# A top-16 search of score columns moved into the query stage of a routed expert layer, and where its row dot products are written

## The chip, the cores and the metric

One core of a Trainium2 chip runs the kernel alone. The metric is the device time of one execution in microseconds, as the median of several runs.

## What is computed

Two transformer-like blocks run over 512 tokens of width 1024. The change lies in the feed-forward part of the first: 8 heads, each with two sets of 128 sub-keys, choose 16 of 16384 one-neuron experts per token.

```python
s1 = einsum('chd,hkd->chk', q[..., :128], keys1)   # scores on 128 keys
s2 = einsum('chd,hkd->chk', q[..., 128:], keys2)
v1, i1 = top_k(s1, 16)
v2, i2 = top_k(s2, 16)
cand = (v1[..., :, None] + v2[..., None, :]).reshape(..., 256)
sc, ci = top_k(cand, 16)
idx = i1[ci // 16] * 128 + i2[ci % 16]
g = softmax(sc)
act = gelu(einsum('chkd,cd->chk', peer_u[idx], h)) * g
out = einsum('chk,chkd->cd', act, peer_v[idx])
```

Everything is float32. A product is formed as three matmuls of operands split into a high and a low part.

## The kernel before

**Tiles and paths.** The tokens form four tiles of 128, t = 0 to 3. Tile 0 takes a sparse path: for each of its 128 (head, choice) pairs an indirect DMA issued by POOL (L1118) gathers one row of `peer_u` per token into a ring of six row tiles, DVE forms the dot product with the token's activations (L1127, a row product and a read of the accumulator), and after a gelu the same is done with rows of `peer_v`, which DVE adds up into `sacc` (L1138). Tiles 1 to 3 (384 tokens) take a dense path through all 16384 experts.

**Stage one, blocks u0 to u127** (`experts_in`). Each block takes 128 experts. SP loads a weight tile `wraw` (512 KB, L225, three buffers), ACT rounds it to `whi` (L268), DVE subtracts to get `wlo` (L269; called the split below), PE does 24 matmuls of 384 columns (L274 to L276), ACT applies the gelu into a tile `A` (L1171), and every second block ACT issues the store of the pair to `adram` (L1173). `A` has three buffers and holds two blocks; eight columns behind them (`hold`) carry the row indices that POOL reads for its gathers.

**Query stage, ahead of u0** (`query`). Sixteen chunks c0 to c15, one per head and half: PE makes a chunk of the queries and then multiplies it with the keys for the four token tiles; ACT copies the scores into `sall` (L1155).

**Routing** (`route(t)`). For each tile: the top 16 of each of 16 score columns, five DVE operations each (L1187 to L1191, called a search below, 64 in all); sums of candidates and their own top 16; softmax; decoding of the indices. For t = 0 the result is `sidx`, the list of rows to gather. For t = 1 to 3 follow 32 items per tile, 96 in all, that make the gate matrix: DVE compares (`O`, L1292) and multiplies twice (L1297), ACT copies, PE does eight matmuls into `pG` (L1301), ACT copies the result into `G` (L1303). After every eighth item ACT stores 2 MB of `G` to `gdram` (L1305).

**Stage two, blocks v0 to v127** (`phase_p2`). `fetch_ag(g)` has SP load 8 blocks of `A` and of `G` (1.5 MB each; `G` shares two buffers with the tiles of the routing). DVE multiplies them (L1341, 128 instructions), ACT and DVE split the product (`ahl`), and PE accumulates it with the rows of `peer_v` in 18 matmuls of 512 columns per block.

**What sets the order.** Every engine works through one static list. A scheduler makes the lists from the order in which the program emits its work, and `phase_p1` sets that by a budget: each u-block adds 4.6 to `have`; the searches and the rest of tile 0's routing take first; once they are done, each block calls `some(1.24)`, which advances the sparse path by 1.24 rows, and then steps of the routing of tiles 1 to 3 until the budget is spent.

```python
have += 4.6
while have > 0 and (d := next(first, None)) is not None:
    have -= d
if have > 0:
    self.some(1.24)
    have -= 1.45
    while have > 0 and left:
        d = next(rest, None)
```

Of the kernel before, what the change touches and what calls it, by code (L numbers as in the profile page):

```python
# [12 lines left out]
F32 = mybir.dt.float32  # L13
# [3 lines left out]
U32 = mybir.dt.uint32  # L17
AF = mybir.ActivationFunctionType
OP = mybir.AluOpType
# [8 lines left out]
TT = S // 128  # L28
SD = S - 128
# [175 lines left out]
class Stream:  # L205
# [38 lines left out]
    def next(self, held=0):  # L244

        n = self.n_used
        self._split(n + 1 + self.ahead - held)
        self.n_used += 1
        return self.got.pop(n)


class Kernel:
# [806 lines left out]
    def phase_p1(self):  # L1059
        nc, pp = self.nc, self.pp  # L1060

        ring = self.p0.tile([128, 4, D], F32, name="ring", tag="xres")
        more = pp.tile([128, 2, D], F32, name="ring2")
        self.ring = [ring[:, j] for j in range(4)] + [more[:, j] for j in range(2)]
        self.hs = pp.tile([128, D], F32, name="hs")
        nc.gpsimd.dma_start(out=self.hs, in_=self.hdram)

        self.iota2 = pp.tile([128, 128, 2], F16, name="iota2")
        nc.vector.tensor_copy(self.iota2, self.iota[:, :, None].to_broadcast([128, 128, 2]))
        self.iota16 = pp.tile([128, 16, 16], BF16, name="iota16")  # L1070
        nc.vector.tensor_copy(self.iota16, self.iota[:, :16, None].to_broadcast([128, 16, 16]))
        self.query()
        self.AG = {}
        first, rest, dense = self.route(0), chain(*(self.route(t) for t in range(1, TT))), self.experts_in()
        self.sparse = self.sparse_experts()

        have = 0.0
        left = True
        for n, _ in enumerate(dense):
            have += 4.6  # L1080
            while have > 0 and (d := next(first, None)) is not None:
                have -= d
            if have > 0:
                self.some(1.24)
                have -= 1.45
                while have > 0 and left:
                    d = next(rest, None)
                    left = d is not None
                    have -= d or 0.0
                have = min(have, 0.0)  # L1090
            if n >= 120 and not left and not self.AG:
                self.fetch_ag(0)
        for _ in chain(first, rest):
            pass
# [8 lines left out]
    def sparse_experts(self):  # L1103

        nc, pp = self.nc, self.pp
        v = nc.vector
        dots = pp.tile([128, 128], F32, name="dots")
        src = [self.a["peer_r"], self.a["peer_v"].rearrange("a b d -> (a b) d")]
        R = len(self.ring)

        def fetch(n):

            if n < 256:
                ix = self.sidx[:, n % 128:n % 128 + 1]
                if n >= R - 1:
                    v.tensor_copy(self.hold[0], ix)  # L1116
                    ix = self.hold.pop(0)
                nc.gpsimd.indirect_dma_start(  # L1118
                    out=self.ring[n % R], out_offset=None, in_=src[n // 128],
                    in_offset=bass.IndirectOffsetOnAxis(ap=ix, axis=0))  # L1120

        for n in range(R - 1):
            fetch(n)
        for n in range(128):
            fetch(n + R - 1)
            r = self.ring[n % R]
            v.tensor_tensor_reduce(r, r, self.hs, 1.0, 0.0, op0=OP.mult, op1=OP.add, accum_out=dots[:, n:n + 1])  # L1127
            yield
        nc.scalar.activation(dots, dots, AF.Gelu)
        v.tensor_tensor(dots, dots, self.sgate, op=OP.mult)  # L1130
        self.sacc = pp.tile([128, D], F32, name="sacc", tag="hs")
        for n in range(128, 256):
            fetch(n + R - 1)
            r, w = self.ring[n % R], dots[:, n - 128:n - 127]
            if n == 128:
                v.tensor_scalar(self.sacc, r, w, None, op0=OP.mult)
            else:
                v.scalar_tensor_tensor(self.sacc, r, w, self.sacc, op0=OP.mult, op1=OP.add)  # L1138
            yield

    def query(self):
        nc, pp = self.nc, self.pp
        keys = self.load(pp, "peer_k", [128, 16, 128], tag="cand")
        self.sall = [pp.tile([128, 2, 16, 128], F32, name="sall", tag="A2", bufs=2) for _ in range(2)]
        for c in range(16):
            if c < 3:
                q = self.q01[c]
            else:
                q = pp.tile([128, S], F32, name="qp", tag="A", bufs=3)
                nc.scalar.copy(q, next(self.xw))  # L1150
            p2 = self.bank("T", (128, TT, 128), "psc")
            for t in range(TT):
                nc.tensor.matmul(p2[:, t], q[:, t * 128:t * 128 + 128], keys[:, c], start=True, stop=True)
            for j in range(2):
                nc.scalar.copy(self.sall[j][:, :, c], p2[:, 2 * j:2 * j + 2])  # L1155

    def experts_in(self):

        nc, pp = self.nc, self.pp
        hi, lo = self.h  # L1160
        for n in range(128):
            w = self.W.next()
            ps = self.mmtile("pl")[:, :SD]
            for k in range(KC):
                ks = slice(k * 128, (k + 1) * 128)
                self.mm3(ps, (w[0][:, ks], w[1][:, ks]), (hi[:, k, 128:], lo[:, k, 128:]), k == 0, k == KC - 1)
            if n % 2 == 0:
                A = pp.tile([128, 2 * SD + 8], F32, name="A", tag="A", bufs=3)
                self.hold = self.places(A, 2 * SD, 8)
                A = A[:, :2 * SD].rearrange("p (j t) -> p j t", j=2)  # L1170
            nc.scalar.activation(A[:, n % 2], ps, AF.Gelu)  # L1171
            if n % 2:
                nc.scalar.dma_start(out=self.adram[n // 8, :, n % 8 - 1:n % 8 + 1], in_=A)  # L1173
            yield 4.0

    def route(self, t):


        nc, pp = self.nc, self.pp
        v = nc.vector  # L1180
        LOW = -3.0e38
        val = pp.tile([128, 16, 16], F32, name="val")
        ix = pp.tile([128, 16, 16], U32, name="ix")
        for c in range(16):
            s = self.sall[t // 2][:, t % 2, c]
            w = pp.tile([128, 128], F32, name="w", bufs=1)
            v.max(val[:, c, :8], s)  # L1187
            v.max_index(ix[:, c, :8], val[:, c, :8], s)
            v.match_replace(w, val[:, c, :8], s, LOW)
            v.max(val[:, c, 8:], w)  # L1190
            v.max_index(ix[:, c, 8:], val[:, c, 8:], w)  # L1191
            yield 1.4

        cand = pp.tile([128, 8, 64], F32, name="cand", tag="sums")
        vv = val.rearrange("p (h i) k -> p h i k", i=2)
# [12 lines left out]
        for h in range(8):  # L1208
            s = cand[:, h]
            w = pp.tile([128, 128], F32, name="w", bufs=1)[:, :64]  # L1210
# [16 lines left out]
        k = pp.tile([128, 3, 8, 16], U32, name="k")  # L1227
# [5 lines left out]
        a, b, p = kf[:, 0], kf[:, 1], kf[:, 2]  # L1233
# [43 lines left out]
        left = pp.tile([128, 32, 4], F32, name="left")  # L1277
# [34 lines left out]
    def fetch_ag(self, g):  # L1312

        nc, pp = self.nc, self.pp
        A = pp.tile([128, 8 * SD + 16], F32, name="A2", tag="A2", bufs=2)
        if g:
# [694 lines left out]
```

## Time and profile before

| | us |
|---|---|
| median of 3 runs | 3414.19 (3411.24 to 3423.83) |
| profiled execution | 3412.77 |
| its span | 3410.5 |
| query stage, first search to the first gelu of u0 | 466 to 555 |
| stage one, gelu of u0 to gelu of u127 | 555 to 1181 |
| between the stages, to the first matmul of v0 | 1181 to 1229.5 |
| stage two | 1229.5 to about 1768 |
| the second block, behind it | to 3410.5 |

| engine | busy us | share of the span |
|---|---|---|
| PE | 3189.3 | 94% |
| DVE | 2349.4 | 69% |
| ACT | 1390.0 | 41% |
| POOL | 956.2 | 28% |

All times of the trace count from the span's start. Shares of the whole span say little on this kernel, because its stages have different limits; the stage at hand is read from stretches and single instructions. Start-to-start spacing of back-to-back instructions is somewhat less than their listed durations, since these overlap.

### The profile page before, as it was taken

To read this page: it belongs to the slowest core of one execution; us is meant where nothing else is said; L and a number is where in the kernel's file an instruction comes from. 1 tells how busy PE (TensorE), PEld (TensorE's weight loads), DVE (VectorE), ACT (ScalarE), POOL (GpSimd) and SP (SyncE) were. 2 spreads that over 40 slices of the span, in tenths; PEclk is the share of its full clock that TensorE was granted. 3 is DMA by queue.
4 is the path that set the end of the run, shared out by engine and by line. 5 is a ranking of instruction groups with operands and counts; after the bars stand their busy time and mean duration, and the time that the engine had idled before them with its cause. 6 is when DMAs were issued, how large, how long until landed. Compare 5 with 4: busy or idle time off the path is not lost.

```text
span 3410.5 us, 46312 instructions
## 1 busy us (share of the span) xinstructions
PE 3189.3 (94%) x17023; PEld 2716.3 (80%) x17023; DVE 2349.4 (69%) x4700; ACT 1390.0 (41%) x2373; POOL 956.2 (28%) x1111
## 2 busy tenths in 40 slices
PE   5988899899999869999999999999999999999998
PEld 5876689899899857777778778888888877888886
DVE  8899546989989867877756874555535784555534
ACT  3334334345455533333334752334422673334421
POOL 5232010433334513223101454311103265131101
PEclk8998899999999979999999999999999999999999
DMA  3332133988889978989743113222334112222322
GB/s 124 99 117 90 56 118 124 344 286 326 319 304 356 341 264 328 347 319 345 279 154 121 38 44 124 87 82 93 99 99 132 60 49 82 87 88 93 99 94 73
DMA packets 173859, 569.79 MB, mean 167 GB/s; under 512 B 18864, under 2 KB 52656, under 8 KB 167616
## 3 DMA queue, kind: packets, MB, share of 16 engines
q1 hardware_dynamic: 114576, 352.37, 30.3%
q0 software_dynamic: 40752, 157.30, 12.5%
q10 hardware_dynamic: 18304, 57.15, 4.3%
q8 instruction: 134, 2.20, 0.3%
q14 instruction: 93, 0.76, 0.1%
HBM read 503.33 MB, written 63.44 MB: 166 GB/s over the span
## 4 chain that ended last, share of the span: by engine, by line
PE 62%; DVE 19%; DMA 10%; issue 4%; POOL 3%; ACT 2%; SPq 0%; DVEq 0%; POOLq 0%; ACTq 0%
PE pl L274 9%; PE pl L275 9%; PE pl L276 9%; DMA wraw<-in_peer_v 4%; DVE wlo L269 3%; DMA ring<-in_peer_r,A 3%; PE mm L274 2%; PE mm L275 2%; PE mm L276 2%; PE acc L275 2%; PE acc L276 2%; PE acc L274 2%; PE T L275 2%; PE T L276 2%; DMA A<-adram 2%
## 5 line engine op out<-in xcount | busy, mean ns | idle before, releaser
L269 DVE TENSOR_TENSOR wlo<-wraw,whi 128x1024 fp32r<-128x1024 f32 x492 | 607.4, 1235 | 547.5 <-ACT whi L268 533.7
L268 ACT CAST whi<-wraw 128x1024 fp32r<-128x1024 f32 x523 | 546.1, 1048 | 865.3 <-PE pl L275 351.3
L276 PE MATMUL pl<-hhi,wlo 128*128 128x384 f32 (+1 forms) x1128 | 389.1, 347 | 14.6 <-DVE wlo L269 14.4
L274 PE MATMUL pl<-hhi,whi 128*128 128x384 f32 (+1 forms) x1128 | 391.4, 347 | 9.3 <-ACT whi L268 9.3
L275 PE MATMUL pl<-hlo,whi 128*128 128x384 f32 (+1 forms) x1128 | 390.0, 346 | 0.0
L275 PE MATMUL pl<-xTlo,whi 128*128 128x512 f32 x944 | 370.3, 392 | 0.0
L274 PE MATMUL pl<-xThi,whi 128*128 128x512 f32 x944 | 369.8, 392 | 0.0
L276 PE MATMUL pl<-xThi,wlo 128*128 128x512 f32 x944 | 367.5, 390 | 0.0
L275 PE MATMUL acc<-wlo,ahl 128*128 128x512 f32 x744 | 294.1, 397 | 0.5 <-DVE wlo L269 0.5
L1118 POOL DMA_INDIRECT ring<-in_peer_v,A x128 | 181.1, 1415 | 393.9 <-DVE A L1116 292.2
L276 PE MATMUL acc<-whi,ahl 128*128 128x512 f32 x744 | 291.1, 395 | 0.0
L274 PE MATMUL acc<-whi,ahl 128*128 128x512 f32 x744 | 236.2, 397 | 26.7 <-ACT ahl L268 16.0
L1118 POOL DMA_INDIRECT ring<-in_peer_r,A x123 | 172.3, 1401 | 296.4 <-DVE A L1116 245.1
L276 PEld LDWEIGHTS pl<-hhi,wlo 128*128 128x128 f32 x1128 | 215.3, 191 | 22.5 <-DVE wlo L269 18.3
L274 PEld LDWEIGHTS pl<-hhi,whi 128*128 128x128 f32 x1128 | 215.6, 191 | 14.9 <-ACT whi L268 11.0
L275 PEld LDWEIGHTS pl<-hlo,whi 128*128 128x128 f32 x1128 | 215.6, 191 | 3.7
L274 PEld LDWEIGHTS pl<-xThi,whi 128*128 128x128 f32 x944 | 177.2, 188 | 38.9 <-issue 0.5
L276 PEld LDWEIGHTS pl<-xThi,wlo 128*128 128x128 f32 x944 | 177.2, 188 | 38.6 <-issue 0.5
L275 PEld LDWEIGHTS pl<-xTlo,whi 128*128 128x128 f32 x944 | 177.4, 188 | 36.8 <-issue 1.0
L274 PEld LDWEIGHTS acc<-whi,ahl 128*128 128x128 f32 x744 | 139.7, 189 | 63.1 <-ACT ahl L268 16.3
L1127 DVE CUSTOM_DVE_ANT_0 ring<-ring,hs 128x1024 f32<-128x1024 f32 x128 | 155.7, 1217 | 38.2 <-DMA ring<-in_peer_r,A 34.4
L1992 POOL TENSOR_TENSOR cv<-cv 128x512 f32<-128x512 f32 x44 | 56.9, 1294 | 430.6 <-ACT cv L1991 430.6
(712 smaller groups left out, 7297.8 us busy)
## 6 DMA issues: line engine op xcount, KB each, us to landing
wraw<-in_peer_u SPq DMA_DIRECT2D x128, 512.0 KB, 6.1
wraw<-in_peer_v SPq DMA_DIRECT2D x128, 512.0 KB, 8.3
wraw<-in_up SPq DMA_DIRECT2D x88, 512.0 KB, 3.3
adram<-A ACTq DMA_DIRECT2D x64, 384.0 KB, 5.9
A<-adram SPq DMA_DIRECT2D x16, 1536.0 KB, 7.3
gdram<-G ACTq DMA_DIRECT2D x12, 2048.0 KB, 11.9
G<-gdram SPq DMA_DIRECT2D x16, 1536.0 KB, 14.3
wraw<-in_down SPq DMA_DIRECT2D x44, 512.0 KB, 3.4
```

Source lines behind the costliest of these rows:

```text
L268: self.nc.scalar.copy(hi, src)
L269: (eng or self.nc.vector).tensor_tensor(lo, src, hi.bitcast(F32), op=OP.subtract)
L274: mm(out, l[0], r[0], start=start, stop=False)
L275: mm(out, l[0], r[1], start=False, stop=False)
L276: mm(out, l[1], r[0], start=False, stop=stop)
L1118: nc.gpsimd.indirect_dma_start(out=self.ring[n % R], out_offset=None, in_=src[n // 128], in_offset=bass.IndirectOffsetOnAxis(ap=ix, axis=0))
L1127: v.tensor_tensor_reduce(r, r, self.hs, 1.0, 0.0, op0=OP.mult, op1=OP.add, accum_out=dots[:, n:n + 1])
L1992: nc.gpsimd.tensor_tensor(ts[0], ts[0], ts[1], op=OP.mult)
```

## The change

The search becomes a function that `query` calls for all four token tiles as soon as a chunk's scores are copied. Its results lie in 32 columns per score column, inside a longer `sall` tile, and `route` reads them there, so that `route` begins with the sums of candidates. The dot products of the sparse path are accumulated into eight further columns behind the current `A` tile (`put`) instead of into `dots`, and one DVE copy per pair of blocks moves them to `dots`. In the budget 4.6 becomes 3.5, `some(1.24)` becomes `some(1.1)` with 1.6 charged for it, and the first `fetch_ag` may be emitted from block 114 on instead of 120.

```diff
@@ phase_p1
+        self.sums = []
...
-            have += 4.6
+            have += 3.5
...
-                self.some(1.24)
-                have -= 1.45
+                self.some(1.1)
+                have -= 1.6
...
-            if n >= 120 and not left and not self.AG:
+            if n >= 114 and not left and not self.AG:
                 self.fetch_ag(0)
@@ sparse_experts
-            v.tensor_tensor_reduce(r, r, self.hs, 1.0, 0.0, op0=OP.mult, op1=OP.add, accum_out=dots[:, n:n + 1])
+            v.tensor_tensor_reduce(r, r, self.hs, 1.0, 0.0, op0=OP.mult, op1=OP.add, accum_out=self.put[:, len(self.sums):len(self.sums) + 1])
+            self.sums.append(n)
             yield
+        self.collect()
@@ query
-        self.sall = [pp.tile([128, 2, 16, 128], F32, name="sall", tag="A2", bufs=2) for _ in range(2)]
+        sall = [pp.tile([128, 2, 32 + 16 * 128], F32, name="sall", tag="A2", bufs=2) for _ in range(2)]
+        self.sall = [s[:, :, 32:].rearrange("p t (c k) -> p t c k", k=128) for s in sall]
+        self.found = [s[:, :, :16 * 128].rearrange("p t (c k) -> p t c k", k=128)[:, :, :, :32] for s in sall]
...
+            for t in range(TT):
+                self.search(t, c)
+    def search(self, t, c):
+        v = self.nc.vector
+        s, f = (x[t // 2][:, t % 2, c] for x in (self.sall, self.found))
+        val, ix = f[:, :16], f[:, 16:].bitcast(U32)
+        w = self.pp.tile([128, 128], F32, name="w", bufs=1)
+        v.max(val[:, :8], s)
+        v.max_index(ix[:, :8], val[:, :8], s)
+        v.match_replace(w, val[:, :8], s, -3.0e38)
+        v.max(val[:, 8:], w)
+        v.max_index(ix[:, 8:], val[:, 8:], w)
+    def collect(self):
+        if self.sums:
+            n, k = self.sums[0], len(self.sums)
+            self.nc.vector.tensor_copy(self.dots[:, n:n + k], self.put[:, :k])
+            self.sums = []
@@ experts_in
             if n % 2 == 0:
-                A = pp.tile([128, 2 * SD + 8], F32, name="A", tag="A", bufs=3)
+                self.collect()
+                A = pp.tile([128, 2 * SD + 16], F32, name="A", tag="A", bufs=3)
                 self.hold = self.places(A, 2 * SD, 8)
+                self.put = A[:, 2 * SD + 8:]
@@ route
-        for c in range(16):
...
-            yield 1.4
+        f = self.found[t // 2][:, t % 2]
+        val, ix = f[:, :, :16], f[:, :, 16:].bitcast(U32)
```

Three places show what the scheduler makes of it. The first is DVE's list in the query stage (`wlo` is the split of a weight chunk, the other rows are operations of searches). Before, two splits of query chunks with what stands between them:

```order
L269 TENSOR_TENSOR wlo<-wraw,whi 128x1024
L1187 MAX val<-sall 128x8
L1188 MAX_INDEX ix<-val,sall 128x8
L1189 MATCH_REPLACE w<-val,sall 128x128
L1190 MAX val<-w 128x8
L1191 MAX_INDEX ix<-val,w 128x8
L1187 MAX val<-sall 128x8
L1188 MAX_INDEX ix<-val,sall 128x8
L1189 MATCH_REPLACE w<-val,sall 128x128
L1190 MAX val<-w 128x8
L269 TENSOR_TENSOR wlo<-wraw,whi 128x1024
```

And in the changed kernel behind a split of the same stage, the first 12 of 28 rows up to the next split:

```order
L269 TENSOR_TENSOR wlo<-wraw,whi 128x1024
L1175 MATCH_REPLACE w<-sall 128x128
L1173 MAX sall<-sall 128x8
L1176 MAX sall<-w 128x8
L1173 MAX sall<-sall 128x8
L1174 MAX_INDEX sall<-sall 128x8
L1177 MAX_INDEX sall<-sall,w 128x8
L1174 MAX_INDEX sall<-sall 128x8
L1175 MATCH_REPLACE w<-sall 128x128
L1176 MAX sall<-w 128x8
L1173 MAX sall<-sall 128x8
L1177 MAX_INDEX sall<-sall,w 128x8
```

What moved: per two chunks two searches stood in the list before and eight stand there now. Ahead of the split of u0 the list held 64 operations of searches and holds 239 of the 320.

The second place is DVE's list at the end of the routing and at the first products of `A` and `G` (L1341, now L1363). Before, all of it behind stage one's last block:

```order
L1292 TENSOR_TENSOR O<-iota_4227,T_9509 128x1024
L1297 TENSOR_TENSOR O<-O,g_9510 128x2x256 x2
L1292 TENSOR_TENSOR O<-iota_4227,T_9509 128x1024 x2
L1297 TENSOR_TENSOR O<-O,g_9510 128x2x256 x4
L1341 TENSOR_TENSOR A_11582<-A_11582,G_11583 128x384 x8
L269 TENSOR_TENSOR ahl<-A_11582,ahl 128x384 x3
L1341 TENSOR_TENSOR A_11858<-A_11858,G_11859 128x384 x8
L269 TENSOR_TENSOR wlo<-wraw,whi 128x1024
```

In the changed kernel, where the first split here is that of u117 and the second that of u118 (L1129 is the dot product with the read of its accumulator, L1118 the copy of an index):

```order
L269 TENSOR_TENSOR wlo<-wraw,whi 128x1024
L1183 COPY dots<-A 128x2
L1363 TENSOR_TENSOR A_11370<-A_11370,G_11371 128x384 x8
L1363 TENSOR_TENSOR A_11870<-A_11870,G_11871 128x384 x8
L1118 COPY A<-sidx 128x1
L269 TENSOR_TENSOR wlo<-wraw,whi 128x1024
L1129 ISA ring,A<-ring,hs 128x1024
L1129 ISA A 128x1
```

What moved: the last `O` stands right behind the split of u112 instead of behind that of v0, the last `pG` matmuls of PE inside block u111 instead of behind u127, and sixteen products stand between the splits of u117 and u118.

The third is SP's list, the queue of the loads (`peer_u` are weights of stage one, `peer_v` of stage two). Before:

```order
L225 DMA wraw<-in_peer_u 128x1024 x25
L225 DMA wraw<-in_peer_v 128x1024 x6
L1321 DMA G_11583<-gdram 128x12x256
L1321 DMA G_11859<-gdram 128x12x256
L1321 DMA G_12111<-gdram 128x12x256
L1321 DMA G_12363<-gdram 128x12x256
L225 DMA wraw<-in_peer_v 128x1024 x5
```

In the changed kernel:

```order
L225 DMA wraw<-in_peer_u 128x1024 x56
L1343 DMA G_11371<-gdram 128x12x256
L1343 DMA G_11871<-gdram 128x12x256
L225 DMA wraw<-in_peer_u 128x1024 x3
L1343 DMA G_12123<-gdram 128x12x256
L1343 DMA G_12375<-gdram 128x12x256
L225 DMA wraw<-in_peer_u 128x1024 x7
```

What moved: the first two loads of `G`, which wait for the last store to `gdram`, stand ahead of the weights of u118, and the next two, which wait for the products of the first, ahead of those of u121.

## Rows read from the trace of the kernel before

**Rows 1.** Busy time by stretch: us, PE, PEld, DVE, ACT, POOL busy, PEclk, DMA share, GB/s.

```profile
465.00:555.00 90.00, 90.00 (x465) 77.57 (x464) 39.77 (x135) 31.78 (x60) 0.00 (x0) 1.00 0.28 94
555.00:612.40 57.40, 57.40 (x334) 57.40 (x333) 51.75 (x218) 26.82 (x35) 8.91 (x8) 1.00 0.59 202
612.40:1180.40 568.00, 532.25 (x3356) 513.97 (x3356) 519.58 (x1390) 271.47 (x409) 221.02 (x150) 0.97 0.89 323
1240.00:1665.00 425.00, 414.38 (x1781) 333.36 (x1780) 328.84 (x484) 146.14 (x197) 121.59 (x96) 1.00 0.89 331
```

**Rows 2.** Waits between 605 and 1030 us: us in total, times, longest.

```profile
DVE ring L1127 <- DMA ring<-in_peer_r,A: 33.3, 21, 7.2
PE pl L276 <- DVE wlo L269: 13.9, 8, 3.4
```

**Rows 3.** Timeline from u127 to v0: start, us, engine, line, operation [idle before <-releaser].

```profile
1180.60 1.10 PE L1301 MATMUL pG<-O,O 128*128 128x128 f16 x16
1180.80 0.49 ACT L1171 ACTIVATE A<-pl 128x384 f32<-128x384 f32 x1 [2.39 <-PE pl L276]
1185.69 1.01 PE L1301 MATMUL pG<-O,O 128*128 128x128 f16 x8 [3.99 <-DVE O L1297]
1214.12 0.33 ACTq L1305 DMA_DIRECT2D gdram<-G  x1
1220.54 1.22 SPq L1321 DMA_DIRECT2D G<-gdram  x2
1228.34 3.84 DVE L1341 TENSOR_TENSOR A<-A,G 128x384 f32<-128x384 f32 x8 [15.89 <-DMA G<-gdram]
1229.50 0.79 PE L274 MATMUL acc<-whi,ahl 128*128 128x512 f32 x1 [16.04 <-ACT ahl L268]
```

**Rows 4.** Busy time in the 25 us around the first matmuls of v0.

```profile
1230.00:1255.00 25.00, 25.00 (x99) 20.07 (x98) 14.79 (x25) 7.69 (x11) 0.00 (x0) 0.89 0.75 237
```

**Rows 5.** Timeline of DVE in the query stage: three searches, then a split and one search.

```profile
466.08 0.29 DVE L1187 MAX8 val<-sall 128x8 f32<-128x128 f32 x1
...
470.07 0.28 DVE L1191 FIND_INDEX8 ix<-val,w 128x8 uint32<-128x128 f32 x1
...
478.43 1.23 DVE L269 TENSOR_TENSOR wlo<-wraw,whi 128x1024 fp32r<-128x1024 f32 x1 [4.21 <-ACT whi L268]
479.57 0.29 DVE L1187 MAX8 val<-sall 128x8 f32<-128x128 f32 x1
...
480.95 0.29 DVE L1191 FIND_INDEX8 ix<-val,w 128x8 uint32<-128x128 f32 x1
```

**Rows 6.** Timeline, the splits of u16 and v0 and the gelu of u16.

```profile
612.39 1.21 DVE L269 TENSOR_TENSOR wlo<-wraw,whi 128x1024 fp32r<-128x1024 f32 x1
621.02 0.49 ACT L1171 ACTIVATE A<-pl 128x384 f32<-128x384 f32 x1 [2.07 <-DMA ring<-in_peer_r,A]
1180.45 1.22 DVE L269 TENSOR_TENSOR wlo<-wraw,whi 128x1024 fp32r<-128x1024 f32 x1
```

**Rows 7.** Lines L1292, L1297, L1138 and L1341 on DVE: ns min/median/max.

```profile
L1292 DVE TENSOR_TENSOR O<-iota,T x96: 669/685/744, 723.5 to 1210.4; 128x1024 f16<-128x1024 f16 x96
L1297 DVE TENSOR_TENSOR O<-O,g x192: 400/418/425, 729.5 to 1212.0; 128x512 f16<-128x512 f16 x192
L1138 DVE SCALAR_TENSOR_TENSOR sacc<-ring,dots,sacc x127: 1271/1280/1315, 1088.0 to 1665.9; 128x1024 f32<-128x1024 f32 x127
L1341 DVE TENSOR_TENSOR A<-A,G x128: 542/551/596, 1228.3 to 1720.0; 128x384 f32<-128x384 f32 x128
```

**Rows 8.** Lines L1305 (stores of G) and L1321 (loads of G): time to landing.

```profile
DMA to landing us min/median/max: 6.3/11.9/12.8
DMA to landing us min/median/max: 7.8/14.3/16.2
```

**Rows 9.** Waits between 1240 and 1665 us.

```profile
PE acc L274 <- ACT whi L268: 10.6, 9, 2.2
```

**Rows 10.** Line L1118, the issues of gathers on POOL: ns min/median/max.

```profile
L1118 POOL DMA_INDIRECT ring<-in_peer_v,A x128: 933/1094/6982, 1076.1 to 1650.4; - x128
L1118 POOL DMA_INDIRECT ring<-in_peer_r,A x123: 932/1234/2935, 607.4 to 1074.8; - x123
```

More of the change, by code (lines that the diff above doesn't have):

```diff
@@ L1106, in sparse_experts @@
         v = nc.vector
-        dots = pp.tile([128, 128], F32, name="dots")
+        dots = self.dots = pp.tile([128, 128], F32, name="dots")
         src = [self.a["peer_r"], self.a["peer_v"].rearrange("a b d -> (a b) d")]
@@ L1181, in route @@
         LOW = -3.0e38
-        val = pp.tile([128, 16, 16], F32, name="val")
-        ix = pp.tile([128, 16, 16], U32, name="ix")
-        for c in range(16):
[L1185 to L1191, printed above, removed]
-            yield 1.4
+        f = self.found[t // 2][:, t % 2]
+        val, ix = f[:, :, :16], f[:, :, 16:].bitcast(U32)
         cand = pp.tile([128, 8, 64], F32, name="cand", tag="sums")
```

## The prediction

> **What bounds the kernel now.** I read the profile in four steps. First, busy time by stretch [rows 1]: in the query stage PE is busy all 90.00 us and DVE 39.77, so PE sets the pace and DVE has some 50 us free. From the split of u16 to that of v0 it is the other way round: DVE is busy 519.58 of 568 us, and PE leaves 568 − 532.25 = 35.8 us unused. Second, the waits [rows 2]: of the long part of that stretch PE waits 13.9 us for splits, while DVE itself waits 33.3 us for gathered rows. DVE is nearly the bound there, though not by much. Third, the timeline from u127 to v0 [rows 3]. The last gelu of stage one is at 1180.80, the first matmul of stage two at 1229.50. In these 48.7 us PE only gets scraps of `pG`, because DVE still works through items of the routing; then come the store of the last 2 MB of `G` (1214.12), its load back (1220.54) and the first product (1228.34, after 15.89 us of waiting for that load). This is the one place where PE has nothing to do, and it exists because DVE is behind with the routing. Fourth, the clock: in the 25 us after it the granted clock is 0.89 [rows 4], so part of them ran at the lower of the two levels, and 0.11 × 25 = 2.7 us are lost.
>
> **Prices.** Back-to-back DVE work starts about 0.08 us before the listed duration is over: a split of 1.23 at 478.43 is followed at 479.57, 1.14 later [rows 5]. Three partly interleaved searches last from 466.08 to 470.07 + 0.28 − 0.08, that is 1.40 each; one alone from 479.57 to 480.95 + 0.21, that is 1.59 [rows 5]. The new list interleaves about as the first, so I take 1.40 and keep 1.59 as the upper bound; fully interleaved, 1.17 is my estimate for the lower one (five operations and two value loads without the gaps). An `O` costs 0.685 − 0.08 = 0.60, a product of it 0.34, a step of `sacc` 1.20, a product of `A` and `G` 0.47 [rows 7].
>
> **Query stage.** Ahead of the split of u0 the list now has 239 operations = 48 searches, 67 us, and 10 splits, 11.4 us. Starting at 466 [rows 5] that ends at 545; PE wants the result about four microseconds ahead of the first gelu at 555, at 550. The searches fill DVE's free time and cost PE nothing: 0, with 1.59 each 4 us. Without that cover (a PE that were faster there) they would cost their full 67. From u0 to u16 the rest follows: 16 searches (22.7), 16 splits (18.4) and 30 more by my count of the list, so the split of u16 comes at 616, against 612.39 before [rows 6]. Before, its block's gelu followed at 621.02 [rows 6], 8.6 us later; 5.4 was the shortest such lag of the trace, so 4 us later costs at most 1. Up to here: nothing gained, with a bound of +12 for slow searches (64 × 0.19).
>
> **Stage one, DVE.** Between the splits of u16 and v0 the two lists differ thus: 37.4 searches out (187 operations), −52.4; 14 `O` and 28 products more, +8.4 and +9.5, since all 96 items now lie in front of v0; 15 `sacc` steps fewer, −18.0; other routing operations 38 fewer at an estimated 0.2, −7.3; 59 copies of dot products less 13 of indices, +3.3 (0.07 each); 16 products of `A` and `G` more, +7.5. Sum −49. Priced so, the list held 555 of the 568 us before (13 idle) and holds 506 now. DVE would be through at 616 + 506 + 13 = 1135.
>
> **Stage one, PE.** PE can't be that fast. A matmul takes 57.40 / 334 = 0.172 us [rows 1], a block 24 × 0.172 = 4.12, an item 1.10 / 2 = 0.55 [rows 3]. Of DVE's 506 us 280 lie before the split of u72, so that comes at 616 + 280 + 7 = 903 and its gelu at 908, with DVE as the bound. From there 55 blocks (227) and 50 items (27.5) are PE's: u127 at 1163. Bounds: with no wait of DVE at all 1151 (616 less the 4 of the query stage, + 280 + 5 + 254); with slow searches (+12) and DVE's waits of 13 doubled, 1193 (616 + 12 + 280 + 26 + 5 + 254).
>
> **Stage one to two.** The last item now stands in u111, so nothing of the routing is left at u127, and the whole wait for items, store and load falls away where it stood. What is late next is the same chain inside stage one. SP's two loads of `G` wait for the store and hold back the weights of u118; DVE waits at the first product with the split of u118 behind it, and needs 16 × 0.47 = 7.5 us for the products. Before, store to product took 1228.34 − 1214.12 = 14.2 us, at a light DMA load [rows 3]. By the medians it is 11.9 + 14.3 = 26.2 [rows 8]. The store leaves at about u112; PE wants the split of u118 some 22 us later. 14.2 + 7.5 is just in time; 26.2 + 7.5 is 12 late. I take 8, and 5 for the scattered late splits that remain of the 13.9 [rows 2]. The first matmul of v0: 1163 + 13 = 1176 against 1229.50, −53.5.
>
> **Stage two.** The clock has no such gap to recover from: −2.7. Of the sparse sum 18 more gathers and steps fall here. One per block, they prolong a state in which PE waits 10.6 us in 425 [rows 9]: 18 × 4.2 × 10.6 / 425 = +2. The reload of the residual and the first transposes behind the sum come later too, two blocks before the end: +2, bounds 0 and 8.
>
> **Sum.** −53.5 − 2.7 + 4 = −52. The profiled execution took 3412.77, so 3361; it stands 1.4 under the median of the runs, so **3362**.
>
> **A rule against it.** Issues of gathers on POOL take 1.1 us in the median, but up to 6.98 us [rows 10], and a long one was read in a stretch of back-to-back DVE work. The Trainium skill, SBUF — State Buffer, section Who interferes with whom, says that a DVE instruction with two SBUF inputs contends with a GpSimd instruction that reads SBUF. By that rule, a DVE rid of its one-input searches and of its gaps would delay the gathers; the rare long issues agree with it, the median doesn't, and by my sum above it is worth nothing.
>
> **Rivals.**
> *DVE stays the bound.* Searches at 1.59 and gathers that make it wait more: for it the 33.3 us of waits [rows 2], against it the smaller number of rows per block (1.1 for 1.24). u127 then comes at about 1193, 30 later than forecast, and the 5 for late splits are in it: 3362 + 30 − 5 = 3387.
> *The chain takes the place of the wait.* Store 12.8, load 16.2 at their longest [rows 8], the second pair of loads waits for the first products and holds back u121's weights, another 16.2, and products 7.5: 53 against the 22 that are covered, 31 where I took 8, and above that if PE falls to its lower clock as it did near 1230 [rows 4], for about 5. Then 3362 + 28 = 3390, up to 3410. Against it: before, store and load were faster.
> *Starved gathers, slower than before.* Each DVE wait for a row holds up the splits behind it. Now 24 waits are 1.6 us each [rows 2]; 142 gathers lie in stage one. v0 would start 17 us later than before if DVE idled 123 us from u16 on (1246 − 616 − 506), so it is decided at 0.87 us per gather. If all waited 1.6, 227 us: v0 at 616 + 506 + 227 + 5 = 1354, 125 later, about 3535. For it: a DMA share of 0.89 [rows 1] and the long issues [rows 10]. Against it: five rows are fetched ahead, some 20 us, and most dots find theirs.
> That the change doesn't do what it says is ruled out by the lists: the searches stand in the query stage.
>
> **How the numbers follow.** The forecast has 0.58, its own range from 3336 (no stall at the loads, no late splits, nothing lost in stage two, no wait of DVE) to 3380. DVE stays the bound 0.22; the chain 0.12; starved gathers 0.08. The range runs from 3335 to 3400: it leaves out half of the chain, the starved gathers and little of the forecast. A difference of 0.5% is about what a measurement of this kernel can tell from none, 3397 and 3431. Faster: 0.58 + 0.21 + 0.05 = 0.84; the same: 0.01 + 0.07 + 0.02 = 0.10; slower: 0.06.
>
> **What would show it.** Right: DVE busy nearly all of the query stage with PE still at 90 of 90; u16's gelu at 620 to 624; u72's near 908; the last `pG` ahead of u112; u127 at 1155 to 1170; no stretch with PE at a few of 25 us; v0 at most 20 us behind u127. Wrong: a query stage longer than 90 us; waits of DVE for gathers above 80 us in stage one; a wait of over 15 us at the first product, with PE waiting for u118's split; waits for the transposes behind the sparse sum of over 10 us.

## The result and the profile after

The changed kernel takes 3357.87 us in the median of four runs (3355.80 to 3360.61), against 3415.85 before on the same chip: a ratio of 0.9827, with an interval of 0.981 to 0.9844. Forecast were 3362 and a range of 3335 to 3400. The profiled execution took 3357.79, its span 3355.5, 55.0 less than before.

Busy time by stretch of the changed kernel (columns as in [rows 1]): the query stage, from the gelu of u0 to the split of u16, from there to the gelu of u16, then from gelu to gelu u16 to u72, u72 to u117 and u117 to u127, the first 50 us of stage two, and its end.

```profile
471.00:561.00 90.00, 90.00 (x466) 77.45 (x465) 87.73 (x464) 31.70 (x60) 0.00 (x0) 1.00 0.27 88
561.00:619.50 58.50, 56.99 (x329) 56.67 (x327) 55.52 (x249) 28.94 (x36) 6.63 (x6) 1.00 0.56 193
619.50:641.80 22.30, 11.80 (x54) 11.80 (x55) 21.79 (x82) 6.01 (x9) 15.50 (x12) 0.69 0.95 350
641.80:903.20 261.40, 258.27 (x1721) 252.11 (x1719) 247.35 (x624) 146.13 (x223) 81.81 (x65) 1.00 0.91 338
903.20:1122.70 219.50, 216.80 (x1480) 209.00 (x1477) 174.64 (x357) 115.35 (x186) 62.97 (x49) 0.99 0.91 338
1122.70:1180.20 57.50, 46.79 (x240) 45.63 (x241) 41.21 (x64) 17.23 (x24) 19.36 (x15) 0.88 0.97 351
1180.20:1230.00 49.80, 49.80 (x217) 40.44 (x216) 43.12 (x56) 17.39 (x25) 14.83 (x12) 1.00 0.88 329
1655.00:1715.00 60.00, 60.00 (x265) 48.74 (x264) 44.61 (x56) 25.11 (x34) 7.06 (x14) 1.00 0.70 248
```

DVE now works 87.73 of the 90 us of the query stage (39.77 before, [rows 1]), and PE still 90.00. Then PE stalls around u12 (11.80 of 22.30 us; the experiments come back to it). From the gelu of u16 to that of u72 it has hardly a gap, 258.27 of 261.40 us. At v0 there is none, as PE's timeline of the changed kernel shows, where the gap of 48.7 us stood in [rows 3]:

```profile
1180.05 0.34 PE L276 MATMUL pl<-hhi,wlo 128*128 128x384 f32 x1
1180.23 0.39 PE L274 MATMUL acc<-whi,ahl 128*128 128x512 f32 x1
```

The chain that filled the gap stands in front of u118 instead. The timeline of the changed kernel, ACT, SP, DVE and PE:

```profile
1096.57 0.33 ACTq L1327 DMA_DIRECT2D gdram<-G  x1
1108.99 3.54 SPq L1343 DMA_DIRECT2D G<-gdram  x2
1112.63 9.16 SPq L225 DMA_DIRECT2D wraw<-in_peer_u  x3
1122.68 3.84 DVE L1363 TENSOR_TENSOR A<-A,G 128x384 f32<-128x384 f32 x8 [7.31 <-DMA G<-gdram]
1126.92 3.84 DVE L1363 TENSOR_TENSOR A<-A,G 128x384 f32<-128x384 f32 x8 [0.39 <-DMA G<-gdram]
1130.74 1.22 DVE L269 TENSOR_TENSOR wlo<-wraw,whi 128x1024 fp32r<-128x1024 f32 x1
...
1122.72 0.49 ACT L1202 ACTIVATE A<-pl 128x384 f32<-128x384 f32 x1 [3.67 <-PE pl L276]
1138.46 0.49 ACT L1202 ACTIVATE A<-pl 128x384 f32<-128x384 f32 x1 [6.98 <-PE pl L276]
...
1129.84 0.69 PE L274 MATMUL pl<-hhi,whi 128*128 128x384 f32 x1 [7.15 <-ACT whi L268]
1132.01 0.69 PE L276 MATMUL pl<-hhi,wlo 128*128 128x384 f32 x1 [1.17 <-DVE wlo L269]
```

Last store 1096.57, loads issued 1108.99, first product 1122.68, split of u118 1130.74; its gelu is 15.7 us behind that of u117, 11.6 more than a block needs. PE waits 8.3 us of these, first for ACT's `whi` of u118, whose weights were issued at 1112.63, behind the first loads of `G`, then for its split, which stands behind the products. The rest is mostly the clock: behind the wait the granted clock is 0.50, the lower of its two levels, as the row of 1132 to 1137 us shows.

```profile
1132.00:1137.00 5.00, 4.99 (x16) 4.99 (x17) 3.60 (x8) 0.00 (x0) 3.77 (x3) 0.50 1.06 318
```

Where the 55.0 us come from, by the two profiled executions: in front of the query stage the changed kernel was 6.2 us later (first search at 472.3 against 466.1), by lists that are the same. From there to the gelu of u127 it won 6.6 (1180.43 against 1180.80, less those 6.2). The gap behind u127 gave 48.9. The first eight blocks of stage two take 32.4 us instead of 35.1, −2.8, which is the clock of [rows 4]. The way from there to the last matmul of stage two (1785.80 before, 1728.38 now) is another 5.4 shorter, and what follows it 2.5 longer. Sum: 6.2 − 6.6 − 48.9 − 2.8 − 5.4 + 2.5 = −55.0.

Of the 5.4, 2.9 are a wait of PE for the reload of the residual, which the changed kernel's order spares (60.00 of 60 us busy above). About 2 more are the clock behind that wait (0.96 and 0.86 granted in the two stretches of 10 us from 1680 us on). Waits between 1660 and 1730 us in the kernel before; the first row is the weight load of the same wait:

```profile
PEld pt L1046 <- DVE xres L944: 3.4, 1, 3.4
PE pt L1046 <- DVE xres L944: 2.9, 1, 2.9
```

### The profile page after: what moved, and what is told of

Same layout as the page of the kernel before. It is cut to its first block, busy times and chain, and to the rows that moved or that the text cites. A ratio compares the mean times of both kernels' runs of the same rounds, so it can differ in the third digit from the quotient of the medians.

```text
span 3355.5 us, 46436 instructions
## 1 busy us (share of the span) xinstructions
PE 3179.3 (95%) x17023; PEld 2712.8 (81%) x17023; DVE 2354.0 (70%) x4759; ACT 1386.1 (41%) x2373; POOL 920.2 (27%) x1111
## 4 chain that ended last, share of the span: by engine, by line
PE 67%; DVE 16%; DMA 9%; POOL 3%; issue 3%; ACT 2%; SPq 0%; DVEq 0%; ACTq 0%; POOLq 0%
PE pl L276 11%; PE pl L274 11%; PE pl L275 11%; DMA wraw<-in_peer_v 5%; DVE wlo L269 3%; PE mm L274 2%; DMA A<-adram 2%; PE mm L275 2%; PE mm L276 2%; PE T L275 2%; PE T L276 2%; PE T L274 2%; PE acc L274 2%; PE acc L276 2%; PE acc L275 2%
## 5 line engine op out<-in xcount | busy, mean ns | idle before, releaser
L276 PE MATMUL acc<-whi,ahl 128*128 128x512 f32 x744 | 287.9, 393 | 0.0
L1120 POOL DMA_INDIRECT ring<-in_peer_v,A x128 | 157.3, 1229 | 385.2 <-DVE A L1118 290.3
L1120 POOL DMA_INDIRECT ring<-in_peer_r,A x123 | 160.4, 1304 | 334.5 <-DVE A L1118 311.3
L274 PE MATMUL acc<-whi,ahl 128*128 128x512 f32 x744 | 226.2, 396 | 10.2 <-ACT whi L268 10.2
L275 PEld LDWEIGHTS acc<-wlo,ahl 128*128 128x128 f32 x744 | 139.9, 188 | 32.2
```

Of the source, the lines that this page charges most:

```text
L274: mm(out, l[0], r[0], start=start, stop=False)
L275: mm(out, l[0], r[1], start=False, stop=False)
L276: mm(out, l[1], r[0], start=False, stop=stop)
L1120: nc.gpsimd.indirect_dma_start(out=self.ring[n % R], out_offset=None, in_=src[n // 128], in_offset=bass.IndirectOffsetOnAxis(ap=ix, axis=0))
```

## The experiments

Ratios are to the kernel before on the same chip; "from u0" means from the gelu of u0, so that what lies ahead of the query stage drops out.

| kernel | median us | lowest, highest | ratio (interval) |
|---|---|---|---|
| the whole change | 3357.87 | 3355.80, 3360.61 | 0.9827 (0.981 to 0.9844) |
| e1 search alone | 3390.27 | 3366.72, 3395.61 | 0.9940 (0.992 to 0.9961) |
| e2 budget alone | 3415.64 | 3405.73, 3425.07 | 1.0006 (0.9991 to 1.0021) |
| e7 columns alone | 3390.27 | 3388.78, 3397.73 | 0.9913 (0.9896 to 0.9929) |
| e3 without the columns | 3387.11 | 3377.75, 3392.04 | 0.9928 (0.9907 to 0.9948) |
| e6 without the budget | 3370.47 | 3366.95, 3373.23 | 0.9853 (0.9837 to 0.9869) |
| e4 sixteen more searches | 3372.36 | 3371.59, 3377.22 | 0.9879 (0.986 to 0.9898) |
| e8 3.2 for 3.5 | 3351.72 | 3348.45, 3359.25 | 0.9809 (0.9791 to 0.9827) |
| e9 3.3 for 3.5 | 3363.46 | 3358.80, 3365.60 | 0.9838 (0.9822 to 0.9854) |
| e10 start at −14 | 3352.88 | 3347.13, 3354.91 | 0.9817 (0.9802 to 0.9833) |
| e11 start at −10, 3.3 | 3354.26 | 3349.17, 3363.12 | 0.9825 (0.9807 to 0.9844) |
| e12 the whole change again | 3358.38 | 3357.93, 3364.25 | 0.9837 (0.9823 to 0.9851) |
| e13 e8 again | 3357.56 | 3351.10, 3359.66 | 0.9829 (0.9814 to 0.9845) |

### Which part brings the gain: e1, e2, e3, e7, e6

e1 is the change without `put` and `collect` and with the old numbers; e2 is the kernel before with the new numbers.

> Only the search moves into the query stage; dot products go to dots as before and the budget keeps 4.6, 1.24, 1.45 and 120. By its lists the last pG stands in u105 (u111 with all of the change), the first loads of G behind the weights of u113, and the dots run 1.24 per block again, so some eight more dots (1.34 us each) and fewer copies lie in DVE's stretch up to u72. Theory: the gain is the end of the routing moving off the stretch between u127 and v0, and the search alone does that: 3357 to 3372 us, the gap between the gelu of u127 and the first matmul of v0 under 10 us, u72 up to 10 us later than with the whole change. Rival (the new budget carries the gain): 3385 us or more.

> Only the four numbers of the budget change (3.5, 1.1, 1.6, 114); the search stays in route and the dots in dots. By its lists the routing still ends behind u127 and 15 fewer steps of sacc lie in stage one. Theory: DVE still has the searches in stage one, so the gap between u127 and v0 stays (40 us or more) and the time is 3395 to 3420 us. Rival (the budget carries the gain): 3375 us or less.

e2 came as the theory said: 3415.64, no difference. e1 did not: 3390.27, the rival's value, though by e2 the numbers alone carry nothing. (The trace of e1 is of its shortest run, 3366.72; the four others lie between 3387.30 and 3395.61, so it does not stand for them.) What e1 lacks besides the numbers are the columns, and e3 takes only those away:

```diff
-            v.tensor_tensor_reduce(..., accum_out=self.put[:, len(self.sums):len(self.sums) + 1])
-            self.sums.append(n)
+            v.tensor_tensor_reduce(..., accum_out=dots[:, n:n + 1])
             yield
-        self.collect()
...
-                self.collect()
-                A = pp.tile([128, 2 * SD + 16], F32, name="A", tag="A", bufs=3)
+                A = pp.tile([128, 2 * SD + 8], F32, name="A", tag="A", bufs=3)
...
-                self.put = A[:, 2 * SD + 8:]
```

> The whole change without the eight columns behind A: dot products go straight to dots and the copies per pair are gone (59 copies of 0.07 us, 4 us of DVE). Theory: the columns matter for nothing but that: 3352 to 3360 us, and the wait of 12 us that PE has for ACT near u12 stays, because it comes from the exponential of the softmax in ACT's list that waits for DVE. Rival: the wait comes from the A tile of an earlier pair being held by dots that are not done, so it falls to under 4 us here, and by the time of u72 nothing of it is left either way. A second rival, that the columns save something (a wait on dots), would make this kernel slower by over 6 us.

3387.11: the second rival. The columns are worth 29 us by the medians and 34 by the ratios (the two kernels ran on different chips), half of the whole gain or a little more, where the theory gave them 4 us of cost. The wait of 12 us near u12 stayed (11.7), so the first rival fell. Where these us lie, the waits of stage one show, first of e3 and then of the changed kernel:

```profile
DVE ring L1129 <- DMA ring<-in_peer_r,A: 49.2, 24, 8.8
```

```profile
DVE ring L1129 <- DMA ring<-in_peer_r,sidx: 2.1, 2, 1.7
```

Without the columns DVE waits 49.2 us for gathered rows (33.3 in a shorter stretch before, [rows 2]), with them it waits for the first two rows only. The timelines show why. e3, dots, index copies for later rows, and one of POOL's gathers:

```profile
705.18 1.22 DVE L1129 CUSTOM_DVE_ANT_0 ring<-ring,hs 128x1024 f32<-128x1024 f32 x1
...
727.58 1.23 DVE L1129 CUSTOM_DVE_ANT_0 ring<-ring,hs 128x1024 f32<-128x1024 f32 x1 [4.55 <-DMA ring<-in_peer_r,A]
729.81 0.20 DVE L1118 COPY A<-sidx 128x1 uint32<-128x1 uint32 x2
...
730.23 9.16 POOL L1120 DMA_INDIRECT ring<-in_peer_r,A  x1 [8.39 <-DVE A L1118]
```

The changed kernel, the same operations:

```profile
707.12 0.15 DVE L1118 COPY A<-sidx 128x1 uint32<-128x1 uint32 x1
707.18 1.22 DVE L1129 CUSTOM_DVE_ANT_0 ring<-ring,hs 128x1024 f32<-128x1024 f32 x1
708.32 0.15 DVE L1118 COPY A<-sidx 128x1 uint32<-128x1 uint32 x1
708.39 1.22 DVE L1129 CUSTOM_DVE_ANT_0 ring<-ring,hs 128x1024 f32<-128x1024 f32 x1
...
707.53 1.67 POOL L1120 DMA_INDIRECT ring<-in_peer_r,A  x1 [4.13 <-DVE A L1118]
709.51 0.93 POOL L1120 DMA_INDIRECT ring<-in_peer_r,A  x1 [0.31 <-issue]
```

A gather needs two things from DVE: the dot that frees its ring slot, and the copy of its index into an `A` tile. In e3 the list has the dots run ahead of the copies. The dot at 705.18 frees the slot for the gather at 730.23, but that row's index is copied only at 729.81, behind a dot (727.58) that itself had to wait 4.55 us for its row; the gather leaves 25 us behind the dot that made room for it. (Its own 9.16 us are the longest issue of this trace, where the median is 1.30.) With the columns a dot writes into the `A` tile too; in the list copy and dot now stand side by side (707.18 and 708.32), and the gather leaves at 709.51. Worked out over all 122 gathers that reuse a slot, from the start of the dot six rows earlier to the issue: 14.4 us in the median for e3, 2.4 for the changed kernel, 10.9 for the kernel before. All ten traces of kernels with the columns have 2.3 or 2.4, the four without them 10.9 to 15.8. The order of DVE's instructions says the same: a dot should find the indices of the six rows from its own on already copied, and with the columns every dot does, while 88 of 122 do not in the kernel before and 45 do not in e3. That the tile is what keeps the dots behind the copies is argued from the lists; that their neighbourhood brings the rows in time is shown, and shown again on the kernel before:

> The kernel before with the dots written behind A and copied per pair, nothing else. Theory: writing a dot into the A tile ties it to that tile, as the index copies are, so that the list sets each index copy right beside the dot that frees its ring slot; the gather goes out some 2 us after that dot instead of 11, DVE's waits for rows in stage one fall from 38 us to under 8, and as DVE is the bound there the time falls by about as much less the copies: 3376 to 3394 us. The gap between u127 and v0 stays above 30 us, because the searches are still in stage one. Rival: the columns only pay together with the search move: 3405 us or more.

e7, the columns alone: 3390.27 against 3418.32 beside it, 28 us, a median of 2.3 us from dot to issue, and 5.6 us of waits for rows. Its u127 comes 598.1 us from u0 (626.0 before), and 53.7 us of gap follow, as the theory said.

> Search in the query stage and dots behind A, but the budget of before (4.6, 1.24, 1.45, 120). By its lists the routing ends in u107 instead of u111 and the rows' dots run 1.24 per block, some eight more of them (1.34 us each, 10 us) before u72, where DVE decides. Theory (search and columns make the gain, the numbers only shift work): 3358 to 3370 us, DVE's waits for gathered rows under 10 us. Rival (the numbers carry a good part of the gain): 3375 us or more.

e6, search and columns with the old numbers: 3370.47, just above the theory's upper end. By the ratios the search alone saves 0.0060 (e1), the columns alone 0.0087 (e7), and both together 0.0147 (e6), which is their sum: each pays without the other. The numbers add 0.0016 (against e12) to 0.0026, with intervals that overlap, so that they add anything is not shown. The fourth number does nothing: with 118, 122 or 125 in place of 114 all lists come out the same.

### Does DVE decide when u72 comes: e4, e10

e4 searches tile 3 twice:

```diff
             for t in range(TT):
                 self.search(t, c)
+            self.search(3, c)
```

> The whole change, with the sixteen searches of tile 3 done twice (the same result written again): 16 x 1.3 to 1.4 = 21 to 22 us more work for DVE in the query stage and the first blocks. Theory: DVE's free time in the query stage is used up and DVE decides when u72 comes, so u16's split and u72 come some 20 us later, and as PE decides from there, the time is 3370 to 3382 us. Rival: DVE has slack again after the change and the work is hidden: under 3363 us.

3372.36, inside the theory's range, 14.5 us more (against a median from another chip) for about 21 us of work: DVE's free time in the query stage is used up. But not by the theory's way. The changed kernel loses time at u12. ACT's timeline there:

```profile
618.91 1.28 ACT L1243 ACT_TABLE_LOAD   x1
626.49 0.31 ACT L1243 ACTIVATE r<-r 128x128 f32<-128x128 f32 x1 [6.29 <-DVE r L1242]
628.17 1.28 ACT L1202 ACT_TABLE_LOAD   x1 [1.37 <-DMA ring<-in_peer_r,A]
629.46 0.87 ACT L1202 ACTIVATE A<-pl 128x384 f32<-128x384 f32 x2
```

The exponential of tile 1's softmax stands in ACT's list ahead of two gelus (u12 and u13) and waits for DVE, which is late with the routing; PE runs out of PSUM buffers and waits. PE's timeline:

```profile
630.00 0.69 PE L274 MATMUL pl<-hhi,whi 128*128 128x384 f32 x1 [12.01 <-ACT A L1202]
```

Behind the wait the granted clock is low too (0.69 from 619.50 to 641.80 above): 54 matmuls take 11.80 us where 0.172 each would be 9.3, so 12.0 + 2.5 make up the 14.6 us by which u16 is late. In e4 u12 comes another 21 us later, all of it in this one wait:

```profile
PE pl L274 <- ACT A L1203: 33.2, 1, 33.2
```

e10 moves that exponential back by four blocks:

```diff
-        have = 0.0
+        have = -14.0
```

> The whole change, with the budget started at -14.0 instead of 0.0. In ACT's list the first exponential of the softmax for tile 1 moves from behind the gelu of u13 to behind that of u17; before it ACT waited 6.3 us for DVE with the gelus behind it, and PE then 12.0 us for a PSUM buffer. The last pG moves from u111 to u114. Theory: the wait of 12 us near u12 falls under 5 us and u16 comes 8 to 14 us earlier, but DVE sets u72, so only a part arrives: 3346 to 3357 us. Rival (the order in ACT's list has nothing to do with it, POOL's late reading of the index columns holds the A tile): u16 unchanged, 3355 to 3364 us.

PE's wait for ACT at u12 is gone, and the exponential now waits 3.37 us, with two gelus behind it (ACT's timeline of e10):

```profile
623.50 0.31 ACT L1243 ACTIVATE r<-r 128x128 f32<-128x128 f32 x1 [3.37 <-DVE r L1242]
627.62 0.87 ACT L1202 ACTIVATE A<-pl 128x384 f32<-128x384 f32 x2
```

These are u16 and u17; by the timelines the exponential went from behind u11 to behind u15, two blocks ahead of where the expectation has it. u12 comes 50.9 us from u0 instead of 68.4, so the rival fell, u16 71.1 instead of 80.8 and u72 331.3 instead of 342.1. The 9.7 us won at u16 are all there at u72. But e10 does not show whether DVE sets u72, because the later start also moves DVE's work behind it: between the splits of u16 and u72 there are five dots and fifteen operations on `O` fewer (instructions of 297.6 us by their durations, 315.0 in the changed kernel), and DVE takes 259.8 us for them instead of 278.2. In the changed kernel both engines arrive together. PE is 99% busy from u16 to u72 (above), and DVE's split of u72 comes 5.4 us ahead of its gelu, the shortest such lag of the trace:

```profile
897.79 1.24 DVE L269 TENSOR_TENSOR wlo<-wraw,whi 128x1024 fp32r<-128x1024 f32 x1
903.21 0.49 ACT L1202 ACTIVATE A<-pl 128x384 f32<-128x384 f32 x1 [0.50 <-PE pl L276]
```

The time of e10 is 3352.88, all five runs under all five of the changed kernel beside it (e12, 3357.93 to 3364.25). It is faster than the kernel before and than the changed kernel.

### What the chain of store, load and product costs: e8, e9, e11, e12, e13

In these the budget of 3.5 is 3.2, 3.3, or 3.3 with a start of −10, so that the routing ends in u127, u121 and u124.

> The whole change with 3.2 for 3.5 in the budget: by its lists the last pG stands in u127, the loads of G and the first products behind stage one, while the number of operations of each engine is the same. Theory: the chain of store, load and product (14 us at the old handover) stands open again between u127 and v0, and the stall of some 16 us around u118 is gone: 3352 to 3370 us. Rival (the chain costs by the medians of 12 and 14 us and the clock falls again): 3371 to 3385 us. If the end of the routing on DVE were what counts, as before, 3390 us or more.

> The whole change with 3.3 for 3.5: by its lists the last pG stands in u121, the first two loads of G stand behind all weights of stage one and the next two three weights later. Theory: the loads of G hold back no weights of u118 to u121, and the store has landed when they are issued, so most of the 16 us around u118 is won and little appears at v0: 3343 to 3356 us. Rival (what stalls there is the DMA engines' own load, 6 MB at 350 GB/s = 17 us wherever they stand): 3356 to 3365 us.

> The same with -10.0 and 3.3 for 3.5: the last pG stands in u124 and the loads of G behind the first four weights of stage two. Theory: both stalls of stage one are gone, and a gap of some 20 us opens at v0 as with 3.2: 3342 to 3356 us. Rival: the gap costs what the stalls did, 3356 to 3364 us.

> The changed kernel as it is, on the same chip as the kernels beside it, so that differences under half a per cent can be told: 3354 to 3362 us.

> The changed kernel with 3.2 for 3.5 once more, beside the changed kernel on the same chip: faster than it by 3 to 9 us if the first run of it (3351.72 against 3357.87 from another chip) was more than the chip. Rival: the same within 2 us.

e8 measured 3351.72, just under the theory's range, e13, the same kernel, 3357.56 beside 3358.38 for the change as it is: the rival, the same within the scatter, so e8's lead was not confirmed. What its trace shows is the chain in the open. ACT and PE of e8:

```profile
1150.97 0.48 ACT L1202 ACTIVATE A<-pl 128x384 f32<-128x384 f32 x1
1174.06 0.79 PE L274 MATMUL acc<-whi,ahl 128*128 128x512 f32 x1 [23.90 <-ACT ahl L268]
```

u127 comes 595.8 us from u0 instead of 619.3, PE waits 23.90, and v0 starts 618.9 from u0 instead of 619.1. All that PE loses ahead of v0 is thus the same with the chain inside stage one and behind it. e9, with the loads at the seam, started v0 at 613.7 from u0, yet took 3363.46: its rival's value, not the theory's. Its trace (of its shortest run, 3358.80) shows where the lead goes. From the first matmul of v0 to that of v8 it needs 43.1 us instead of 32.4, with PE waiting another 5.1 us for weights behind the second pair of loads, and the granted clock is 0.79 in the 30 us from 1170 on:

```profile
1170.00:1200.00 30.00, 23.79 (x81) 18.16 (x82) 24.03 (x27) 8.31 (x13) 11.11 (x7) 0.79 0.87 318
```

So the loss moved with the loads. Whether it is the waits for the loads or the DMA engines' own load, as the rival has it, is not told apart by these runs. e11 came to 3354.26, in the theory's range, with a gap of 16.5 us at v0; its runs, 3349.17 to 3363.12, cover the rival's range too.

## Why the prediction came out

**Query stage: right.** PE's 90.00 us stayed. From 472.3 to the split of u0 at 546.32 lie 48 searches and 10 splits: (74.0 − 11.4) / 48 = 1.30 each, under the 1.40 taken.

**u16: wrong.** "4 us later costs at most 1" looked at splits alone. The split was even early (619.56, 613.4 without the 6.2, for 616), but the gelu came 14.6 later than before (641.84 − 621.02 − 6.2), by way of ACT's list and PE's PSUM buffers. e10, which takes the stall away and shifts other work as well, ends 5.5 us earlier.

**u16 to u72: fair size, and both engines the bound.** "With DVE as the bound" gave 908 for u72, 914 with the 6.2 in front; it came at 903.21. From the split of u16 to that of u72 DVE took 278 us (280 + 7 forecast) and came just in time, 5.4 us ahead of the gelu. PE, which the forecast gave slack here, had none left after the stall at u12.

**The columns: the step that failed.** They entered the sum as copies, +3.3, with DVE's idle time kept at 13. Nothing in the prediction says that this idle time hung on them. Nor is 13 the idle time of the trace: the lists priced at 555 and 506 us were busy for 519.6 and 480.8, and before the change DVE waited 38.2 us for rows alone (24 waits, 21 of them in [rows 2]). With the columns 2.1 remain. Without them DVE waits 49 us for rows and the time is 3387.11. This is the figure of the rival "DVE stays the bound", by its waits alone, as the searches did not take 1.59. The lists, with copy and dot side by side, would have shown it: the price of 0.07 us was right, the place in the list was worth some 29 us. So half of the gain is the columns' and about a third the search's (0.0087 and 0.0060 of 0.0173), where the forecast gave it to the search.

**Stage one to two: right.** 13 us of stalls were put behind the loads of G and late splits; 57.5 us for ten blocks of 4.12 are 16 more than needed. From store to first product it took 26.1 us, as by the medians (26.2), and not 14.2; the first product waited 7.31 us, u118 was 11.6 late (8 taken, 12 as the bound). About 5.6 of the 16 are not waits but slower matmuls (PE busy 46.79 us at a granted clock of 0.88, 41.2 needed): the lower clock that the forecast named only in its rival on the chain. v0 began at 1180.23, 1174 without the 6.2: forecast 1176.

**Stage two: clock right, tail of the wrong sign.** The clock gave 2.8 at v0, though it now falls at u12 (0.69 over 22 us) and at u118 (0.50 over 5 us). The +4 for a later sparse sum became −5.4: the transposes now stand 518 us behind the first matmul of v0 in PE's timeline instead of 458, and PE no longer waits for them.

**The total: in part luck.** Without the 6.2, u16 was 14.6 late, the way from u16 to u72 some 26 shorter than forecast (261.4 for 287) and the way from u72 to v0 9 longer (277.0 for 268). The errors cancel to 2 us at v0. And the idle time stayed small only because of the columns: without them the same sum would come out some 3 us lower, and e3 lies 27 us above the upper end that its expectation drew from it. Of the signs named beforehand DVE's and PE's busy time in the query stage, the last `pG` and v0 came true; u16's gelu (635.6 for 620 to 624), u72's (897.0 for 908) and u127 (1174.2 for 1155 to 1170) did not. The forecast's own lower end, 3336, is 3333 by the terms it names.

**The rule against it.** The mean issue of a gather went from 1401 and 1415 ns to 1304 and 1229, by the pages' groups of L1118 and L1120. The rule of the Trainium skill (SBUF — State Buffer, section Who interferes with whom), that a DVE instruction with two SBUF inputs contends with a GpSimd instruction that reads SBUF, would have lengthened them if DVE had been busier; no run here shows that it cost time. It is no test of the rule, for between the splits of u16 and v0 DVE was busy 480.8 of 554.6 us, 87%, against 91% before. Starved gathers did decide some 29 us, but through the order of DVE's list, and in favour of the change.

## What to carry to other kernels

A busy engine's later work can be put where an earlier stage leaves it free, if its inputs are there; look for that by stretch, and then in every engine's list for what stands behind the work that was moved (here an exponential on ACT). For a prefetch, list all instructions that release it and how far apart they stand: it leaves only when the last of them is through, and an edit that costs nothing may put them together or pull them apart. A chain of store, load and use that is moved under other work still has to be covered: with the chain inside stage one and with it open at its end, stage two started 619.1 and 618.9 us from u0.

## What was not expected of the hardware

Two executions of the changed kernel agree within 0.3 us from u0 to u117 (561.6 and 561.7 us), while the way to the first search, by the same list, took between 465.4 us (e1) and 473.7 (e11) in the fourteen traces. The granted clock between 360 and 380 us goes with it: 0.83 in the two traces under 466.2 us, 0.74 to 0.79 in the four from 466.4 to 468.8, 0.67 to 0.70 in the eight above 471. It was 0.83 before and 0.69 after. Differences of a few us between single profiles are best read from a mark inside the stage in question.
